# Two of the four weight sums of the last up block and of all down units, made by memory-to-memory transfers during the up product

## The chip, the cores and the metric

One core of a Trainium2 chip runs the whole kernel in one launch. The metric is device time in microseconds; lower is better. Three runs of the kernel before took 2117.33, 2120.94 and 2121.91 us, so the median is 2120.94 us.

## The reference, cut to what matters

The program is one decoder block on 512 rows of 2048 channels, in float32: a norm, an input projection, two token mixers, an output projection, and then the channel mixer, which is all that the change touches:

```
h   = rmsnorm(x) * norm2_g                 # 512 x 2048
up  = h @ ffn_w_up                         # 2048 x 12288
up  = causal depthwise conv, width 3       # per column
gate, val = split(up)
x   = x + (gelu(gate) * val) @ ffn_w_down  # 6144 x 2048
out = rmsnorm(x) * final_g
```

## The kernel before, in words

**Products.** Each matrix product of the channel mixer is cut into 2 x 2 blocks and done with seven block products in place of eight. A "unit" is one step of it: a weight block of 2 x 128 rows by 512 columns against the matching part of the activations. A unit makes seven products (`ORDER`, `SLOTS`), each in two halves of the rows and in three passes (high by high, high by low, low by high part), so 42 matmuls in line 782. 24 up blocks of 8 units (192 units, `ups`) come first, gate and value by turns, and then 88 down units: `CHUNKS` of 8, 8 and 6 row pairs, each for four column groups `n`. A last piece of the down product (two row pairs, `TAIL`) is done plainly at the end.

**What a weight needs.** A tile `q` has eight slots of 128 x 256. A weight's four quarters are loaded into slots 4 to 7 by one transfer of 512 KB from SyncE's queue, SP (`Weights.load`, line 581). VectorE then makes four sums (`Weights.sums`): slots 2 and 3 in one instruction (line 585: slots 5 and 6, each plus slot 7), slot 1 (line 586: slot 2 plus slot 6), slot 0 (line 587: slot 1 plus slot 4). Then `pair` splits slots 0 to 6 into a high and a low part: ScalarE casts (line 115), VectorE subtracts (line 116). An activation tile goes the same way (`Acts`, lines 604, 610 to 612, and line 116 as `al`); in the down product it is read back from `ad`, an array in device memory to which the value blocks write their result (line 850, from GpSimd, POOL).

**What sets the order.** From line 755 on the program order is the order of each engine. `stream` lists weights and activations in the order of use; `prepare` walks it. For entry n it issues load n+1, makes the sums of n+1, pairs n, and issues load n+2; `ready` sets it to run two units ahead of the product. `q`, the high parts and the low parts have three buffers each. So load e+3 waits on SP until VectorE has finished the pair of entry e, and between that moment and the sums of e+3 VectorE has the sums of e+2, the pair of e+1 and whatever `lazy` work lies between. `lazy` work is hung on later units by `later`: after an up block the seven `combine` steps at its end and the convolution steps of `rest` (lines 845, 848) in the units +1, +2, +4 and +5 of the next block; after a down block three sums out of PSUM (lines 895, 898, 900) at its end and pairs of `steps` (lines 902 to 909) in the units +0 to +3 of the next.

**Activations of the down product.** They are entries of the same stream, at spread-out places around each start of a chunk (`spread`, `after`): 8 for the first chunk, in units 187 to 199 counted from the first up unit, 8 in 219 to 231, 6 in 251 to 260, each prepared about two units earlier.

**POOL** issues few transfers: the writes to `ad`, and in the down product the reads and writes of the residual `xs` to and from `x2d` (lines 886 and 922, 1 MB each). Each waits in POOL's queue for what it writes.

Of the kernel before, what the change touches and what calls it, by code (L numbers as in the profile page):

```python
# [8 lines left out]
F32 = mybir.dt.float32  # L9
# [3 lines left out]
ALU = mybir.AluOpType  # L13

P = 128
# [31 lines left out]
CHUNKS = [range(0, 8), range(8, 16), range(16, 22)]  # L47
TAIL = 22
# [16 lines left out]


@with_exitstack
def hybrid_block(ctx: ExitStack, tc: tile.TileContext, x, xT, w_in, w_out, w_up, w_dn, w_dl, wab, wsT, vec, bs, vgb, fg, out):
    nc = tc.nc
    const = ctx.enter_context(tc.tile_pool(name="const", bufs=1))  # L70
    def pool(name, side, bufs=1):
# [2 lines left out]
    def psum(name, bufs):  # L74
        return tc.alloc_tile_pool(name=name, bufs=bufs, space=bass.MemoryType.PSUM, reuse_waits="tile")
# [34 lines left out]
    def col(at):  # L110
        return vc[:, at:at + 1]
# [43 lines left out]
    def sl(pair, *idx):  # L155
        return tuple(t[idx] for t in pair)
# [54 lines left out]
    def rms_rstd(dst, sums, width, n):  # L211

        m = sums.shape[-1]
        v = mx.tile([P, n], F32, name="rms_v", tag="rms_v", bufs=2)
        if m > 1:
            nc.vector.tensor_reduce(v, sums, mybir.AxisListType.X, ALU.add)
            sums = v
        else:
            sums = sums[:, :, 0]
        nc.vector.tensor_scalar(v, sums, 1.0 / width, RMS_EPS, ALU.mult, ALU.add)  # L220
        rsqrt(dst, v)
# [348 lines left out]
    def slots(name, n=8):  # L570
        return wq.tile([P, n, 256], F32, name=name, tag=name)

    class Weights:


        def __init__(self, src):
            self.src = src

        def load(self):
            self.q = slots("q")  # L580
            nc.sync.dma_start(self.q[:, 4:8], self.src)

        def sums(self):
            q = self.q
            nc.vector.tensor_tensor(q[:, 2:4], q[:, 5:7], q[:, 7:8].broadcast_to([P, 2, 256]), ALU.add)  # L585
            nc.vector.tensor_tensor(q[:, 1], q[:, 2], q[:, 6], ALU.add)  # L586
            nc.vector.tensor_tensor(q[:, 0], q[:, 1], q[:, 4], ALU.add)  # L587

# [52 lines left out]
    stream = []  # L641
# [4 lines left out]
    def rest_of_loads():  # L646
        while halves:
            halves.pop(0)()

    def prepare(upto, last=None):  # L650

        last = len(stream) - 1 if last is None else last
        for n in range(done[2], upto + 1):

            for i, step, ahead in ((0, "load", 1), (1, "sums", 1), (2, "pair", 0), (0, "load", 2)):
                for k in range(done[i], min(n + ahead, last) + 1):
                    if step == "sums":
                        rest_of_loads()
                    getattr(stream[k], step)()
                    done[i] = k + 1  # L660

    ups = [(g, v) for g in range(NG) for v in range(2)]
    units = [(w_up[g + NG * v, m], m) for g, v in ups for m in range(8)]
    starts = []
    for c in CHUNKS:
        starts.append(len(units))
        units += [(w_dn[n, p], p - c[0]) for n in range(4) for p in c]
    n_up = starts[0]

    def act_tiles(m, shape):  # L670
        a = pools["a2" if m == 7 else "a1"]
        return tuple(a.tile(shape, F32R, name=f"a{n}{m}", tag=f"a{n}{m}") for n in "hl")
# [46 lines left out]
    last_w = [Plain([w_dl[d].rearrange("p (a b) -> p a b", a=8)], half_tiles(i)) for i, d in enumerate(DORD)]  # L719
    for u, (src, _) in enumerate(units):  # L720
        place[u] = len(stream)
        stream.append(Weights(src))
        for a in after.get(u, ()):
            if a.fill is not None:
                a_place[a.m] = len(stream)
            stream.append(a)
        if u == len(units) - 5:
            stream.append(last_a)
        if u == len(units) - 2:
            stream.append(last_w[0])  # L730
    stream += last_w[1:]

    def ready(u):

        if u < 7:
            return a_place[u + 1 if u else 0]
        n = len(units)
        return place[u + 3] - 1 if u + 3 < n else place[n - 1] + max(0, u - n + 2)
# [33 lines left out]
    def product(q, p, a, w, up, first, last):  # L772
        sa, sb = SLOTS[p]
        if first:
            q[p] = qbank().rearrange("p (t n) -> p t n", t=2)
        for t in range(2):
            s, r = ((w, sb), (a, sa)) if up else ((a, sa), (w, sb))
            sh, slo = (h[:, s[1], t * P:(t + 1) * P] for h in s[0])
            rh, rlo = (h[:, r[1]] for h in r[0])
            for n, (x_, y_) in enumerate(((sh, rh), (sh, rlo), (slo, rh))):  # L780

                nc.tensor.matmul(q[p][:, t], lhsT=x_, rhs=y_, start=first and t == 0 and n == 0, stop=last and t == 1 and n == 2, skip_group_check=True)  # L782
# [3 lines left out]
    def later(step, f):  # L786
        lazy.setdefault(step, []).append(f)

    def t_tile(name, shape, bufs=1):
        return pools["t"].tile(shape, F32, name=name, tag=name, bufs=bufs)  # L790
# [4 lines left out]
    def combine(q, c1, c11, c12, c21, c22):  # L795

        tt = nc.vector.tensor_tensor
        nc.scalar.copy(c1, q[1])
        tt(c11, c1, q[2], ALU.add)  # L799
        v, w = t_tile("v", [P, 2, 256]), t_tile("w", [P, 2, 256])  # L800
        tt(v, q[6], c1, ALU.subtract)
        tt(w, q[5], v, ALU.add)
        tt(c12, w, q[3], ALU.add)
        tt(c22, w, q[7], ALU.add)
        tt(v, v, q[7], ALU.add)
        tt(c21, q[4], v, ALU.subtract)
# [3 lines left out]
    def up_block(g, val, u0):  # L810
        q = {}
        for m in range(8):
            prepare(ready(u0 + m))
            for p in ORDER:
                product(q, p, act[m], stream[place[u0 + m]].hl, True, m == 0, m == 7)
                if p == 6:
                    rest_of_loads()
            if m == 7 and u0 == 0:
                pads[:] = [t_tile(f"pad{n}", [P, 2, S + 2]) for n in range(2)]
                for t in pads:  # L820
                    nc.gpsimd.memset(t[:, :, 0:2], 0.0)
            for f in lazy.pop(u0 + m, ()):
                f()
        c1 = t_tile("c1", [P, 2, 256])
        lo, hi = slice(2, 258), slice(258, 514)
        combine(q, c1, pads[0][:, :, lo], pads[1][:, :, lo], pads[0][:, :, hi], pads[1][:, :, hi])
        if u0 == 0:
            pools["ps"].release()
            pools["tr"].release()
            pools["ps"] = psum("q1", 8)  # L830

        def tap(n, j, f):
            if val:
                dst = t_tile("cv", [P, 2, S])if j == 0 else cvs[n]
                cvs[n] = dst
            else:
                if j == 0:
                    gates[n] = t_tile("gate", [P, 2, S], 2)
                dst = gates[n]
            nc.scalar.activation(dst[:, j], pads[n][:, j, 2:2 + S], AF.Identity, bias=col(V_FB + f), scale=col(V_FW + 2 * 96 + f))  # L840

        def rest(n, j, f):
            dst = (cvs if val else gates)[n][:, j]
            for i in (1, 0):
                nc.vector.scalar_tensor_tensor(dst, pads[n][:, j, i:i + S], col(V_FW + i * 96 + f), dst, ALU.mult, ALU.add)
            if val:
                gate = gates[n][:, j]
                nc.vector.tensor_tensor(gate, gate, dst, ALU.mult)
                at = 0 if j else 2
                nc.gpsimd.dma_start(ad[2 * g + n][:, at:at + 2], gate.rearrange("p (a b) -> p a b", a=2))  # L850

        def gelu(n, j):
            t = gates[n][:, j]
            nc.scalar.activation(t, t, AF.Gelu_apprx_tanh)

        cvs = {}
        at = u0 + 8
        for i, (n, j) in enumerate(((1, 0), (1, 1), (0, 0), (0, 1))):
            f = 48 * val + 4 * g + 2 * n + j
            step = at + (0, 1, 3, 4)[i]  # L860
            later(step, lambda n=n, j=j, f=f: tap(n, j, f))
            later(step + 1, lambda n=n, j=j, f=f: rest(n, j, f))
            if not val:
                later(step + 2, lambda n=n, j=j: gelu(n, j))

    pads = []
    for b, (g, val) in enumerate(ups):
        up_block(g, val, 8 * b)
# [69 lines left out]
    for st in range(NS):  # L938
# [4 lines left out]
        for n, (i, d, lo, hi) in enumerate(pieces):  # L943
            ps = qbank()[:, 0:hi - lo]
            for f in range(4):
                at = (0 if f % 2 else 1024 // 2) + st * P
                a = sl(last_a.hl[f // 2], slice(None), slice(at, at + P))
                w = sl(last_w[i].hl[f // 2], slice(None), slice(f % 2 * 512 + lo, f % 2 * 512 + hi))
# [12 lines left out]
        v, y, u, r = (const.tile([P, 1], F32, name=f"r3{c}", tag=f"r3{c}", bufs=2) for c in "vyur")  # L961
# [7 lines left out]
        for n in order:  # L969
            _, d, lo, hi = pieces[n]  # L970
# [64 lines left out]
```

## Time and profile before

| | us |
|---|---|
| three runs | 2117.33, 2120.94, 2121.91 |
| median | 2120.94 |
| profiled execution | 2120.2 |
| its span | 2118.5 |
| TensorE busy | 2052.5 (97%) |
| VectorE busy | 1807.7 (85%) |
| ScalarE busy | 910.6 (43%) |
| GpSimd busy | 59.7 (3%) |

The profiled execution lies 0.7 us under the median, and 1.7 us of it lie around the span. Sums are made against it. The mean granted clock of TensorE was 0.985 of full speed (2.4 GHz). A matmul's duration is modelled and matmuls overlap in the pipeline, so the pace of line 782 is read from counts over a stretch, not from the duration of one.

### The profile page before, as it was taken

How to read it: one execution, taken by the hardware profiler on the slowest of the kernel's cores; microseconds unless marked ns; L12 is line 12 of the kernel's file. 1: busy time of each engine (PE TensorE's matmuls, PEld its weight loads, DVE VectorE, ACT ScalarE, POOL GpSimd, SP SyncE). 2: the span in 40 equal slices, each digit the busy share in tenths (PEclk: the TensorE clock that was granted, in tenths of full speed). 3: DMA queues.
4: the chain of work that ended last, by engine and by line, in shares of the span. 5: the costliest groups of instructions: out<-in, count | busy, mean ns of one | idle time of the engine just before them, and what ended most of it. 6: DMA issues, size and time to landing. Idle time of an engine off the chain costs nothing.

```text
span 2118.5 us, 34519 instructions
## 1 busy us (share of the span) xinstructions
PE 2052.5 (97%) x14488; PEld 1931.3 (91%) x14488; DVE 1807.7 (85%) x2345; ACT 910.6 (43%) x899; POOL 59.7 (3%) x118
## 2 busy tenths in 40 slices
PE   9999999999889999999999999999988998999998
PEld 7888888888689999999999999999988998998996
DVE  7588972745389999999999999999999999989986
ACT  6445322413264444444444444444444344444443
POOL 0000000100000000000000000000000000000000
PEclk9999999999899999999999999999999999999999
DMA  6222322434123443333333333333335454544563
GB/s 236 87 90 90 102 97 99 159 124 158 57 70 103 127 125 105 129 116 115 120 123 115 121 113 118 120 118 122 113 120 177 151 181 168 178 150 160 199 214 125
DMA packets 68604, 275.12 MB, mean 130 GB/s; under 512 B 8160, under 2 KB 8800, under 8 KB 58720
## 3 DMA queue, kind: packets, MB, share of 16 engines
q1 hardware_dynamic: 57888, 224.01, 32.6%
q0 software_dynamic: 9984, 48.24, 6.1%
q8 instruction: 113, 1.85, 0.4%
q10 hardware_dynamic: 576, 0.66, 0.1%
q14 instruction: 43, 0.35, 0.1%
HBM read 241.43 MB, written 31.46 MB: 129 GB/s over the span
## 4 chain that ended last, share of the span: by engine, by line
PE 80%; DVE 15%; DMA 3%; ACT 1%; issue 1%; SPq 0%; DVEq 0%; ACTq 0%
PE qs L782 52%; PE ps L153 9%; PE ps L151 9%; PE ps L152 9%; DVE wl L116 5%; DVE al L116 2%; DVE q L585 1%; DMA q<-w_dn 1%; DVE q L586 1%; DVE q L610 1%; DVE q L587 1%; DMA q<-w_up 1%; PE qs L152 1%; PE qs L153 1%; PE qs L151 1%
## 5 line engine op out<-in xcount | busy, mean ns | idle before, releaser
L782 PE MATMUL qs<-ah,wh 128*128 128x256 f32 x2688 | 764.6, 284 | 3.1 <-DVE pad L799 1.9
L782 PE MATMUL qs<-ah,wl 128*128 128x256 f32 x2688 | 763.2, 284 | 4.3 <-DVE wl L116 4.3
L782 PE MATMUL qs<-al,wh 128*128 128x256 f32 x2688 | 763.5, 284 | 2.9 <-DVE al L116 2.7
L115 ACT CAST wh<-q 128x1792 fp32r<-128x1792 f32 (+1 forms) x282 | 476.8, 1691 | 669.9 <-PE qs L782 472.6
L116 DVE TENSOR_TENSOR wl<-q,wh 128x1792 fp32r<-128x1792 f32 (+1 forms) x282 | 567.5, 2013 | 25.0 <-ACT wh L115 24.8
L782 PEld LDWEIGHTS qs<-ah,wl 128*128 128x128 f32 x2688 | 518.5, 193 | 4.7 <-DVE wl L116 4.7
L782 PEld LDWEIGHTS qs<-al,wh 128*128 128x128 f32 x2688 | 518.7, 193 | 3.7 <-DVE al L116 3.7
L782 PEld LDWEIGHTS qs<-ah,wh 128*128 128x128 f32 x2688 | 518.6, 193 | 3.7 <-DVE pad L799 2.1
L782 PE MATMUL qs<-wl,ah 128*128 128x256 f32 x1232 | 355.8, 289 | 16.1 <-DVE wl L116 16.0
L782 PE MATMUL qs<-wh,ah 128*128 128x256 f32 x1232 | 355.1, 288 | 9.1 <-ACT cc L894 3.5
L782 PE MATMUL qs<-wh,al 128*128 128x256 f32 x1232 | 354.4, 288 | 4.7 <-DVE al L116 4.7
L782 PEld LDWEIGHTS qs<-wl,ah 128*128 128x128 f32 x1232 | 242.5, 197 | 18.4 <-DVE wl L116 18.3
L782 PEld LDWEIGHTS qs<-wh,ah 128*128 128x128 f32 x1232 | 242.5, 197 | 10.5 <-ACT cc L894 3.9
L782 PEld LDWEIGHTS qs<-wh,al 128*128 128x128 f32 x1232 | 242.3, 197 | 5.1 <-DVE al L116 5.1
L116 DVE TENSOR_TENSOR wl<-wraw,wh 128x1024 fp32r<-128x1024 f32 (+2 forms) x105 | 118.0, 1125 | 147.1 <-ACT wh L115 146.8
L115 ACT CAST wh<-wraw 128x1024 fp32r<-128x1024 f32 (+2 forms) x105 | 102.2, 974 | 275.1 <-PE ps L152 145.3
L585 DVE TENSOR_TENSOR q<-q 128x512 f32<-128x512 f32 x280 | 191.6, 684 | 14.6 <-DMA q<-w_dn 13.1
L151 PE MATMUL ps<-xgh,wh 128*128 128x512 f32 x384 | 152.4, 397 | 0.6 <-ACT wh L115 0.5
L152 PE MATMUL ps<-xgl,wh 128*128 128x512 f32 x384 | 152.1, 397 | 0.0
L153 PE MATMUL ps<-xgh,wl 128*128 128x512 f32 x384 | 150.5, 397 | 0.0
L586 DVE TENSOR_TENSOR q<-q 128x256 f32<-128x256 f32 x280 | 119.0, 425 | 9.7
L587 DVE TENSOR_TENSOR q<-q 128x256 f32<-128x256 f32 x280 | 119.1, 425 | 9.6
(242 smaller groups left out, 2285.2 us busy)
## 6 DMA issues: line engine op xcount, KB each, us to landing
q<-w_up SPq DMA_DIRECT2D x192, 512.0 KB, 3.5
q<-w_dn SPq DMA_DIRECT2D x88, 512.0 KB, 3.5
wraw<-w_in SPq DMA_DIRECT2D x28, 1024.0 KB, 4.9
wraw<-w_out SPq DMA_DIRECT2D x16, 1024.0 KB, 4.9
ad<-gate POOLq DMA_DIRECT2D x48, 256.0 KB, 2.3
q<-ad SPq DMA_DIRECT2D x24, 512.0 KB, 3.2
xs<-x2d POOLq DMA_DIRECT2D x12, 1024.0 KB, 5.9
x2d<-xs POOLq DMA_DIRECT2D x10, 1024.0 KB, 5.1
```

Source lines behind the costliest of these rows:

```text
L115: nc.scalar.copy(h, src)
L116: nc.vector.tensor_tensor(l, src, h.bitcast(F32), ALU.subtract)
L151: nc.tensor.matmul(ps, lhsT=ah, rhs=bh, start=start, stop=False)
L152: nc.tensor.matmul(ps, lhsT=ah, rhs=bl, start=False, stop=False)
L153: nc.tensor.matmul(ps, lhsT=al, rhs=bh, start=False, stop=stop)
L585: nc.vector.tensor_tensor(q[:, 2:4], q[:, 5:7], q[:, 7:8].broadcast_to([P, 2, 256]), ALU.add)
L586: nc.vector.tensor_tensor(q[:, 1], q[:, 2], q[:, 6], ALU.add)
L587: nc.vector.tensor_tensor(q[:, 0], q[:, 1], q[:, 4], ALU.add)
L610: nc.vector.tensor_tensor(q[:, 2:4], q[:, 7:8].broadcast_to([P, 2, 256]), q[:, 5:7], ALU.subtract)
L782: nc.tensor.matmul(q[p][:, t], lhsT=x_, rhs=y_, start=first and t == 0 and n == 0, stop=last and t == 1 and n == 2, skip_group_check=True)
```

## The change

For the eight weights of the last up block (units 184 to 191) and the 88 of the down product, slots 2 and 3 are no longer made by line 585. The host hands over a second copy of the operands as `w_us` and `w_ds`: for each weight two arrays of 256 KB, one with the quarters of slots 5 and 6, one with the quarter of slot 7 twice. `make(u)`, called once in each up unit u from 0 to 191, issues one transfer from POOL, memory to memory, of 32 rows of 8 KB: for even u a copy of the first array into `made`, for odd u the second array added to what is there. After two up units the sums of one weight are done; 96 weights take 192 units. Such a weight is then loaded by two transfers, 256 KB of `made` into slots 2 and 3 (2 KB a partition) and 384 KB of the quarters into slots 4 to 6 (3 KB a partition), where one transfer of 512 KB was (4 KB a partition). Lines 586 and 587 and the pair stay as they are.

```diff
-            self.q = slots("q")
-            nc.sync.dma_start(self.q[:, 4:8], self.src)
+            self.q = q = slots("q")
+            if self.made is None:
+                nc.sync.dma_start(q[:, 4:8], self.src)
+            else:
+                nc.sync.dma_start(q[:, 2:4], self.made)
+                nc.sync.dma_start(q[:, 4:7], self.src[:, 0:3])
 
         def sums(self):
             q = self.q
-            nc.vector.tensor_tensor(q[:, 2:4], q[:, 5:7], q[:, 7:8].broadcast_to([P, 2, 256]), ALU.add)
+            if self.made is None:
+                nc.vector.tensor_tensor(q[:, 2:4], q[:, 5:7], q[:, 7:8].broadcast_to([P, 2, 256]), ALU.add)
             nc.vector.tensor_tensor(q[:, 1], q[:, 2], q[:, 6], ALU.add)
             nc.vector.tensor_tensor(q[:, 0], q[:, 1], q[:, 4], ALU.add)
...
+    sums_src = [w_us[m] for m in range(8)] + [w_ds[n, p] for c in CHUNKS for n in range(4) for p in c]
+    for k, src in enumerate(sums_src):
+        made[n_up - 8 + k] = tc.dram_tile([32, 2048], F32, name=f"made{k}")
+
+    def make(u):
+
+        k = u // 2
+        if k < len(sums_src):
+            how = {"accum_op": ALU.add, "max_dma_last_dim": 8192} if u % 2 else {"max_dma_last_dim": 8192}
+            nc.gpsimd.dma_start(made[n_up - 8 + k], sums_src[k][u % 2], **how)
...
                 if p == 6:
                     rest_of_loads()
+            make(u0 + m)
             if m == 7 and u0 == 0:
...
+        "w_us": pairs(i["ffn_w_up"][0])[23],
+        "w_ds": pairs(i["ffn_w_down"][0][:TAIL * 2 * P]),
```

## Rows read from the trace of the kernel before

**Rows 1.** Section 1 of the page: busy time, share of the span and instructions of each engine.

```profile
PE 2052.5 (97%) x14488; PEld 1931.3 (91%) x14488; DVE 1807.7 (85%) x2345; ACT 910.6 (43%) x899; POOL 59.7 (3%) x118
```

**Rows 2.** Busy time of line 782 alone, over the whole of both block products: stretch, its length, PE busy (matmuls), PEld busy (weight loads), granted clock, DMA share, GB/s.

```profile
474.00:2065.00 1591.00, 1439.08 (x11760) 1431.33 (x11760) 0.98 0.41 133
```

**Rows 3.** The same for stretches from the last two up blocks to the end of the down units, PE only: stretch, length, PE busy (matmuls), granted clock, DMA share, GB/s.

```profile
1526.00:1576.00 50.00, 44.18 (x351) 0.97 0.37 117
1576.00:1642.00 66.00, 56.33 (x414) 0.90 0.47 160
1642.00:1713.00 71.00, 70.79 (x590) 1.00 0.51 172
1713.00:1813.00 100.00, 89.06 (x702) 0.97 0.49 168
1813.00:1890.00 77.00, 76.68 (x639) 1.00 0.50 165
1890.00:1967.00 77.00, 69.83 (x554) 0.96 0.46 151
1967.00:2063.00 96.00, 95.93 (x787) 0.98 0.61 209
```

**Rows 4.** Busy time of every engine in a stretch within the up product: stretch, length, PE (matmuls), PEld, DVE, ACT, POOL, granted clock, DMA share, GB/s.

```profile
700.00:900.00 200.00, 200.00 (x1669) 200.00 (x1668) 192.23 (x244) 90.67 (x75) 5.42 (x10) 1.00 0.38 119
```

**Rows 5.** VectorE's groups by line: the sums of a weight and the low part of its pair (busy us, mean ns of one, idle time before).

```profile
L116 DVE TENSOR_TENSOR wl<-q,wh 128x1792 fp32r<-128x1792 f32 (+1 forms) x282 | 567.5, 2013 | 25.0 <-ACT wh L115 24.8
L585 DVE TENSOR_TENSOR q<-q 128x512 f32<-128x512 f32 x280 | 191.6, 684 | 14.6 <-DMA q<-w_dn 13.1 <-DMA q<-w_up 0.8
L586 DVE TENSOR_TENSOR q<-q 128x256 f32<-128x256 f32 x280 | 119.0, 425 | 9.7
```

**Rows 6.** VectorE in order of time, early in the last up block: start us, duration us, what.

```profile
1537.89 0.69 DVE L585 TENSOR_TENSOR q<-q 128x512 f32<-128x512 f32 x1
1538.62 0.43 DVE L586 TENSOR_TENSOR q<-q 128x256 f32<-128x256 f32 x1
1539.08 0.43 DVE L587 TENSOR_TENSOR q<-q 128x256 f32<-128x256 f32 x1
1539.42 2.02 DVE L116 TENSOR_TENSOR al<-q,ah 128x1792 fp32r<-128x1792 f32 x1
1541.36 1.53 DVE L845 SCALAR_TENSOR_TENSOR gate<-pad,vc,gate 128x512 f32<-128x512 f32 x2
1542.81 0.68 DVE L585 TENSOR_TENSOR q<-q 128x512 f32<-128x512 f32 x1
```

**Rows 7.** Pieces of the chain that ended last which are loads, from the last up block to the end of the third chunk's start: start us, us, what.

```profile
1571.66 3.45 DMA q<-w_dn
1608.67 3.65 DMA q<-w_dn
1630.63 7.95 DMA q<-w_dn
1642.21 17.90 PE qs L782 x147
...
1746.53 5.31 DMA q<-ad
1800.61 5.22 DMA q<-w_dn
...
1933.49 3.57 DMA q<-w_dn
```

**Rows 8.** DMA queues (packets, MB, share of 16 engines' span) and issues (KB each, median us from issue to landing).

```profile
q1 hardware_dynamic: 57888, 224.01, 32.6%
q0 software_dynamic: 9984, 48.24, 6.1%
q<-w_dn SPq DMA_DIRECT2D x88, 512.0 KB, 3.5
wraw<-w_in SPq DMA_DIRECT2D x28, 1024.0 KB, 4.9
```

**Rows 9.** SP's queue in order of time: one weight load (start us, us that it held the queue).

```profile
1554.73 0.33 SPq L581 DMA_DIRECT2D q<-w_up  x1
```

**Rows 10.** VectorE in order of time in the middle of the up product, one step of a gate block's convolution and what follows it: start us, duration us, what.

```profile
1300.75 1.53 DVE L845 SCALAR_TENSOR_TENSOR gate<-pad,vc,gate 128x512 f32<-128x512 f32 x2
1302.19 0.69 DVE L585 TENSOR_TENSOR q<-q 128x512 f32<-128x512 f32 x1
1302.91 0.42 DVE L586 TENSOR_TENSOR q<-q 128x256 f32<-128x256 f32 x1
1303.38 0.42 DVE L587 TENSOR_TENSOR q<-q 128x256 f32<-128x256 f32 x1
1303.72 2.02 DVE L116 TENSOR_TENSOR wl<-q,wh 128x1792 fp32r<-128x1792 f32 x1
1305.65 0.68 DVE L585 TENSOR_TENSOR q<-q 128x512 f32<-128x512 f32 x1
```

**Rows 11.** POOL in order of time: the last write of the residual ahead of the up product, the first clearing in it, and a write of a value block's result (start us, us, what, idle time before it and what ended that).

```profile
563.14 0.53 POOL L560 DMA_DIRECT2D x2d<-x  x1 [21.23 <-DVE x L520]
595.00 0.14 POOL L821 MEMSET pad<- 128x4 f32 x2 [31.33 <-PE tr L688]
...
1499.19 0.54 POOL L850 DMA_DIRECT2D ad<-gate  x1 [59.75 <-DVE gate L848]
```

More of the change, by code (lines that the diff above doesn't have):

```diff
@@ L67, in hybrid_block @@
 @with_exitstack
-def hybrid_block(ctx: ExitStack, tc: tile.TileContext, x, xT, w_in, w_out, w_up, w_dn, w_dl, wab, wsT, vec, bs, vgb, fg, out):
+def hybrid_block(ctx: ExitStack, tc: tile.TileContext, x, xT, w_in, w_out, w_up, w_dn, w_us, w_ds, w_dl, wab, wsT, vec, bs, vgb, fg, out):
     nc = tc.nc
@@ L573, in hybrid_block, with __init__ @@
     class Weights:
-        def __init__(self, src):
-            self.src = src
+        def __init__(self, src, made=None):
+            self.src, self.made = src, made
         def load(self):
-            self.q = slots("q")
-            nc.sync.dma_start(self.q[:, 4:8], self.src)
+            self.q = q = slots("q")
[4 more added lines that the diff above has]
+                nc.sync.dma_start(q[:, 4:7], self.src[:, 0:3])
         def sums(self):
             q = self.q
-            nc.vector.tensor_tensor(q[:, 2:4], q[:, 5:7], q[:, 7:8].broadcast_to([P, 2, 256]), ALU.add)
+            if self.made is None:
+                nc.vector.tensor_tensor(q[:, 2:4], q[:, 5:7], q[:, 7:8].broadcast_to([P, 2, 256]), ALU.add)
             nc.vector.tensor_tensor(q[:, 1], q[:, 2], q[:, 6], ALU.add)
@@ L664, in hybrid_block @@
     starts = []
+    made = {}
     for c in CHUNKS:
@@ L721, in hybrid_block @@
         place[u] = len(stream)
-        stream.append(Weights(src))
+        stream.append(Weights(src, made[u].rearrange("(p b) (c d e) -> (p b c) d e", p=32, c=4, d=2) if u in made else None))
         for a in after.get(u, ()):
@@ L1002, in quarters, with pairs @@
         return c(np.stack([b[:, :, :, 0, 1], b[:, :, :, 0, 0], b[:, :, :, 1, 1], b[:, :, :, 1, 0]], axis=3))
+    def pairs(w):
+        q = quarters(w)
+        return c(np.stack([q[:, :, :, 1:3], q[:, :, :, [3, 3]]], axis=2)).reshape(*q.shape[:2], 2, 32, 2048)
     vec = np.concatenate(
```

## The prediction, made before the changed kernel was seen

> **What bounds the kernel now.** I read the page's engine line first, then line 782 over stretches, then the chain, and last VectorE (DVE) and the queues in order of time. The engine line gives PE 97% and DVE 85% [rows 1], an average that hides the stage concerned. Line 782 has 11760 matmuls in the 1591 us of both block products [rows 2], 42 for each of 280 units. In the middle of the up product 1669 of them pass in 200 us without a gap [rows 4]: 0.120 us each, 5.04 us a unit. That stage is bound by PE, yet DVE is busy 192.2 of the 200 us, so it has 3.9% to spare, 3.1 us in 16 units (80.6 us).
>
> By the same pace I read what each later stretch loses: its length less its matmuls times 0.12 [rows 3]. 1526 to 1576: 50 - 42.1 = 7.9. 1576 to 1642: 66 - 49.7 = 16.3. 1713 to 1813: 100 - 84.2 = 15.8. 1890 to 1967: 77 - 66.5 = 10.5. Together 50.5 us; the stretches between them lose under 2 us each. The four losing stretches are three places, A, B and C, the starts of the three chunks, where activations of the down product go through DVE beside the weights. In them the chain runs along DVE, broken by loads [rows 7]. The granted clock is 1.00 (the 2.4 GHz level) where PE never waits, and 0.90 in mean in the stretch where it waits longest.
>
> **What the change removes.** 96 executions of line 585 at 684 ns [rows 5], 65.7 us of DVE. In sequence one is worth 0.72 us, the step from its start to that of line 586 [rows 6]. The sums of a weight then take 0.80 us in place of 1.53 (to the start of the pair, same rows), a pair 1.94. Only sums made while DVE sets the end count: by the order of `prepare`, 16 weights in A (units 187 to 202), 16 in B (219 to 234), 12 in C (251 to 262), so 44 x 0.72 = 31.7 us. The other 52 free DVE time where PE sets the pace: nothing.
>
> **What takes part of it back: the load.** Three buffers of `q` mean that load e+3 starts when the pair of e ends, and DVE reaches the sums of e+3 after one lot of sums and one pair, plus whatever lazy work lies between. Without lazy work that was 1.53 + 1.94 = 3.47 us, and the load there takes 3.45 to 3.65 [rows 7]: they are balanced to a tenth. After the change DVE is there in 2.74 us (3.47 if the sums between are an activation's), and the load is bigger: 640 KB in two transfers.
>
> The length of the new load, L, no row shows. Lower end, bytes alone: 1024 KB land in 4.9, 512 KB in 3.5 [rows 8], so 128 KB more cost 0.35: 3.45 + 0.35 = 3.8. Upper end, packets alone: a load of 1024 KB makes as many packets (224 MB in 57888 is 3.9 KB each [rows 8], so 256) as two transfers of 128 partitions; with the second issue, 0.33 us on SP [rows 9], 4.9 + 0.33 = 5.2. Ours has 256 packets of 2 and 3 KB, nearer to the bytes; the first transfer's data covers the second's issue. I take 4.1.
>
> The Trainium skill (DMA: Bandwidth & Descriptors, Anatomy of one DMA) fits a transfer as about 2.0 us plus bytes over 436 GB/s; as an estimate from it 128 KB more cost 0.3, L is 3.75 and the gain would be 21.6 before the deductions below. The rows' slope, 0.35, is a little steeper.
>
> Now the waits, by walking entry by entry through A, B and C. A window holds at least 1.2 us of lazy work in most units, and 2.74 + 1.3 = 4.04 covers L. Not covered are six weights with bare windows (194, 196, 199; 224, 234; 256), each L - 2.74 = 1.36, together 8.2; four whose window holds an activation's sums (188, 225, 232, 257), each L - 3.47 = 0.63, together 2.5; three that follow directly on a weight that waited (226, 233, 258), 0.72 each, and one activation, loaded in 3.45 against 2.74, 0.7: together 2.9. Sum 13.6 us. 31.7 - 13.6 = 18.1: about 6.1 in A, 6.0 in B, 5.9 in C, each below what that place loses, so PE can take it.
>
> **Smaller terms.** Loads beside 1 MB transfers of `xs` take 5.2 to 8.0 us [rows 7]. Two weight loads there grow by 0.4 and their sums shrink by 0.7; two activation loads (the one shown in B and its like in C) are the same and DVE reaches them 0.7 sooner, which is lost. Net 1 us lost. SP issues 96 more transfers of 0.33 us, hidden in the 2.7 us between two loads.
>
> **POOL.** It gains 192 issues of about 0.54 us [rows 11], 104 us, and is idle 97%. The addition waits in its queue for the copy to land. By issue 0.54, landing up to 3.5 and issue 0.54 a weight takes some 5 us, so eight in 16 units hold it 40 of 80 us. Queued behind are the writes to `ad`, delayed by up to one such wait, 4 us; their `gate` buffers are wanted again six units (30 us) later. The clearing of the pads stands behind the first eight transfers; POOL has 31 us between the write at 563 and the clearing [rows 11] and needs 20. Without that cover (over 8 us a weight) the first block starts late by the excess, once. A `made` of unit 184 + k is finished by unit 2k + 1, and its load is asked for about unit 181 + k: never late.
>
> **The up product.** The transfers share the 16 DMA engines with weight loads there. Per engine a copy is 16 KB; q0 moved 48.24 MB in 6.1% of 16 engines' span and q1 224.01 MB in 32.6% [rows 8], 43 and 49 us x engine per MB, so 0.7 to 0.8 us. For an addition no row exists: from nothing beyond a copy (0.75), if reading its target is hidden, to three passes (2.4). I take two, 1.5. A load of 3.45 beside it becomes 4.95. The shortest window in an up block is sums, pair and one step of 1.45: 1302.19 - 1300.75 + 3.46 = 4.9 us [rows 10]; in a value block 5.6. So an addition just fits, and the 3.1 us to spare absorb the rest; with jitter I charge 1 to 2 us.
>
> The Trainium skill (DMA: Bandwidth & Descriptors, Issuing engines are not separate DMA queues) speaks against the change here: transfers of all queues interleave on the same 16 engines. It gives no price for an addition, and no row of this trace shows one.
>
> **Sum.** 18.1 - 1 - 2 = 15 us. The profiled execution took 2120.2, 0.7 below the median of the runs: 2105 there, 2106 as a median.
>
> **Rivals.**
> 1. The load takes all of it. With one transfer more and 256 packets L may be 4.8 or more. Then the windows with lazy work no longer cover: 6 x 2.06 + 4 x 1.33 + 2.9 = 20.6, and about 17 windows of 4.1 lose 0.7 each, 11.9: 32.5, the whole gain. The time is 2121. At L = 5.2 it is about 11 us worse. For it: balance already at 3.45, so any growth counts double. Against it: small packets. Chance 0.18.
> 2. Contention in the up product: slower. If an addition holds an engine 2.4 us, a load beside it takes 5.85, DVE waits 0.95 in a window of 4.9, and PE, with only 3.1 us of DVE time to spare per 16 units, is passed. Eight additions in 16 units: 7.6 - 3.1 = 4.5, in some 11.5 such stretches 52 us; less the 17 gained, 2155. It decides from about 2.0 us an addition: 8 x 0.55 - 3.1 = 1.3, times 11.5 is 15. For it: DVE is 96% busy there; after each four `ad` writes POOL runs ahead, so transfers bunch. Against: the stage's DMA share is only 0.38 [rows 4], and `prepare` runs two units ahead. Chance 0.20.
> 3. The loads stay at 3.45. Then waits are 6 x 0.71 + 2.9 = 7.2, the gain 24.5, and with a steadier clock in A up to 30: 2096, at best 2090. For it: both transfers are in flight together. Against: more bytes. Chance 0.15.
>
> **How the numbers follow.** The forecast, 2098 to 2116, has 0.47. An 80% range takes in rivals 3 and 1 and the near end of rival 2: 2090 to 2132. About 0.2% (4 us) is what a measurement of this kernel can tell from no change. Faster by over that: 0.47 + 0.15 less 0.03 of the forecast's edge, 0.59. Within: 0.13 of rival 1, 0.03 of the edge and 0.01 of rival 2's mild forms: 0.17. Slower: 0.19 of rival 2 and 0.05 of rival 1: 0.24.
>
> **What would show it.** In the changed profile line 585 runs 184 times. Weight loads of the down units land about 4.1 us after the first issue. DVE's idle time on those loads in A to C grows from 13 us [rows 5] to some 20 to 25, and the matmuls of A to C take 18 us less. In the up product PE stays at 1669 matmuls in 200 us. I am wrong if PE falls below that (rival 2), or if the chain in A to C is made of loads (rival 1).

## The result, and the profile after

The changed kernel took 2107.73 us as a median of four runs (2103.72 to 2108.02) against 2120.68 for four of the kernel before: ratio 0.9935, 95% interval 0.9923 to 0.9948. Two later sets of five gave 0.9925 (0.9913 to 0.9938) and 0.9937 (0.9924 to 0.9951). The forecast was 2106 as a median; the profiled execution took 2107.67 where 2105 was forecast.

The engine line, which answers to [rows 1]:

```profile
PE 2048.9 (97%) x14488; PEld 1928.0 (92%) x14488; DVE 1746.8 (83%) x2249; ACT 911.5 (43%) x899; POOL 185.9 (9%) x310
```

DVE has 96 instructions and 61 us less, POOL 192 instructions and 126 us more. The product line, 782 before, is line 800 now; over the whole of both block products, as in [rows 2]:

```profile
474.00:2053.00 1579.00, 1435.05 (x11760) 1428.07 (x11760) 0.98 0.56 173
```

The stretches that answer to [rows 3] (length, PE busy and matmuls, granted clock, DMA share, GB/s), cut at the same points of the chain:

```profile
1528.00:1576.00 48.00, 43.07 (x355) 1.00 0.65 190
1576.00:1624.00 48.00, 40.15 (x291) 0.88 0.47 157
1624.00:1717.00 93.00, 93.00 (x757) 0.97 0.58 205
1717.00:1805.00 88.00, 78.94 (x632) 0.98 0.59 202
1805.00:1890.00 85.00, 85.00 (x708) 1.00 0.54 188
1890.00:1957.00 67.00, 63.82 (x515) 0.97 0.54 189
```

Length less 0.12 us a matmul: 5.4, 13.1, 12.2 and 5.2 in the four losing stretches, 35.9 us where [rows 3] gave 50.5. The middle of the up product, as in [rows 4], with all transfers running:

```profile
700.00:900.00 200.00, 200.00 (x1669) 200.00 (x1669) 191.96 (x245) 89.44 (x74) 34.22 (x54) 1.00 0.63 175
```

The same 1669 matmuls, though the DMA share went from 0.38 to 0.63. VectorE's groups, as in [rows 5] (line 590 was 585, 591 was 586), and its idle time by what ended it, 1520 to 2060 us (engine, line, what it waited for: us in total, times, longest):

```profile
L590 DVE TENSOR_TENSOR q<-q 128x512 f32<-128x512 f32 x184 | 126.1, 685 | 6.4 <-DMA q<-w_up 6.2
```

```profile
DVE wl L116 <- ACT wh L115: 44.1, 37, 3.0
DVE q L591 <- DMA q<-w_dn: 20.1, 18, 3.1
DVE q L615 <- DMA q<-ad: 6.6, 5, 2.5
DVE q L591 <- DMA q<-w_up: 3.1, 3, 1.7
...
DVE xs L914 <- DMA xs<-x2d: 1.4, 1, 1.4
```

The same view of the kernel before:

```profile
DVE q L585 <- DMA q<-w_dn: 13.1, 12, 2.8
DVE wl L116 <- ACT wh L115: 9.5, 8, 3.0
DVE q L610 <- DMA q<-ad: 2.5, 2, 2.1
```

So waits on loads went from 15.6 us in 14 places to 31.2 in 27. Not all of that was given back: a wait of VectorE costs time only in the starts, and TensorE (PE) runs without a gap from 1624 to 1717 and from 1805 to 1890 us. The same view of the changed kernel for the three starts alone (1528 to 1624, 1717 to 1805 and 1890 to 1957 us):

```profile
DVE q L591 <- DMA q<-w_dn: 3.3, 4, 1.5
DVE q L591 <- DMA q<-w_up: 2.5, 2, 1.7
DVE q L615 <- DMA q<-ad: 1.2, 1, 1.2
...
DVE q L591 <- DMA q<-w_dn: 7.5, 4, 3.1
DVE q L615 <- DMA q<-ad: 2.7, 2, 2.1
...
DVE q L615 <- DMA q<-ad: 2.7, 2, 2.5
DVE q L591 <- DMA q<-w_dn: 1.9, 2, 1.1
```

And of the kernel before (1526 to 1642, 1713 to 1813 and 1890 to 1967 us):

```profile
DVE q L585 <- DMA q<-w_dn: 3.0, 2, 2.8
...
DVE q L585 <- DMA q<-w_dn: 3.0, 2, 1.7
DVE q L610 <- DMA q<-ad: 0.5, 1, 0.5
...
DVE q L610 <- DMA q<-ad: 2.1, 1, 2.1
DVE q L585 <- DMA q<-w_dn: 0.2, 1, 0.2
```

In the starts the waits went from 8.8 us in 7 places to 21.8 in 17: 13.0 us given back. The waits on line 115, ScalarE's cast, went from 9.5 to 44.1 us, and 42.8 of these lie between the starts and behind the last. There the cast in its turn waits for a buffer that TensorE still reads:

```profile
1717.00 1.69 ACT L115 CAST wh<-q 128x1792 fp32r<-128x1792 f32 x1 [3.35 <-PE qs L800]
...
1718.72 2.03 DVE L116 TENSOR_TENSOR wl<-q,wh 128x1792 fp32r<-128x1792 f32 x1 [0.29 <-ACT wh L115]
```

So most of what the sums outside the starts took, 52 x 0.72 = 37 us, became idle time of VectorE. The chain shows the loads, as in [rows 7]; here are pieces from the last up block to the second start, with the issue of the first of the two transfers in the line ahead of a load:

```profile
1535.74 0.33 SPq L584
...
1536.11 4.63 DMA q<-w_up
...
1552.78 4.76 DMA q<-ad
...
1572.95 0.32 SPq L584
...
1573.31 3.35 DMA q<-w_dn
...
1588.12 3.19 DMA q<-w_dn
...
1608.61 3.70 DMA q<-w_dn
...
1742.59 7.56 DMA q<-ad
...
1795.85 6.12 DMA q<-w_dn
```

Beside the transfers a load here took 5.0 us from its first issue (1535.74 to 1540.74). Once the last of them, issued at 1552, is over, the loads shown in A take 3.6 to 4.1 (1572.95 to 1576.66 is 3.7). The last two lines, in B, are loads beside the 1 MB transfers of the residual.

The gain can be laid out by unit: the start of every 42nd matmul of the product line, in order of time, in us later (+) or earlier (-) than in the profiled execution of before.

```
unit      0      12     184    204    236    268    last
after   -0.05  +2.84  +2.84  -1.04  -5.07  -12.02  -12.02
```

Up product, units 0 to 184, +2.9, A (184 to 204) -3.9, B (to 236) -4.0, C (to 268) -7.0, what follows the last unit -0.5: -12.5 in the span.

### The profile page after: what moved, and what is told of

Read it like the earlier page. It is cut to its first block, busy times and chain, and to the rows that moved or that the text cites. A ratio compares the mean times of both kernels' runs of the same rounds, so it can differ in the third digit from the quotient of the medians.

```text
span 2106.0 us, 34882 instructions
## 1 busy us (share of the span) xinstructions
PE 2048.9 (97%) x14488; PEld 1928.0 (92%) x14488; DVE 1746.8 (83%) x2249; ACT 911.5 (43%) x899; POOL 185.9 (9%) x310
## 4 chain that ended last, share of the span: by engine, by line
PE 84%; DVE 10%; DMA 4%; issue 1%; ACT 1%; SPq 0%; DVEq 0%; ACTq 0%
PE qs L800 56%; PE ps L153 9%; PE ps L152 9%; PE ps L151 9%; DVE wl L116 3%; DVE al L116 2%; DMA q<-ad 1%; DMA q<-w_dn 1%; DMA q<-w_up 1%; DVE q L591 1%; DVE q L615 1%; PE qs L152 1%; PE qs L153 1%; PE qs L151 1%; DVE q L592 0%
## 5 line engine op out<-in xcount | busy, mean ns | idle before, releaser
L800 PEld LDWEIGHTS qs<-wh,ah 128*128 128x128 f32 x1232 | 240.9, 196 | 12.2 <-ACT cc L913 4.9
L591 DVE TENSOR_TENSOR q<-q 128x256 f32<-128x256 f32 x280 | 118.6, 424 | 29.7 <-DMA q<-w_dn 20.1
L686 POOL DMA_DIRECT2D made<-w_ds x176 | 115.3, 755 | 283.0 <-DMA made<-w_ds 273.8
L590 DVE TENSOR_TENSOR q<-q 128x512 f32<-128x512 f32 x184 | 126.1, 685 | 6.4 <-DMA q<-w_up 6.2
```

Source lines behind the costliest of these rows:

```text
L686: nc.gpsimd.dma_start(made[n_up - 8 + k], sums_src[k][u % 2], **how)
```

## Experiments

Theory A: the removed sums are worth their 0.72 us each in the three starts, less what VectorE then waits for longer loads; the transfers cost only where VectorE is late, in the first up block and in the last. Rivals are named with each run.

**1. No transfers.** The two slots come straight from the first operand array.

```diff
-            make(u0 + m)
-        made[n_up - 8 + k] = tc.dram_tile([32, 2048], F32, name=f"made{k}")
+        made[n_up - 8 + k] = src[0]
```

> Leaves out the memory-to-memory transfers: the two slots are loaded straight from the first operand array, so the product of the last up block and of the down units is not the reference's. Loads (two, 640 KB) and VectorE work are those of the changed kernel (2107.7). Theory A (the transfers cost something only where VectorE is late: the first two up blocks, 2.8 us, and the last up block, where loads took 4.8 to 5.1 us): 2102, with the shift of the first up blocks gone and some 3 us more gained in A. Rival B (the transfers are hidden, and what is missing of the 31.7 us is lost to the loads alone): 2107 to 2108.

2105.07 us, ratio 0.9920 (0.9905 to 0.9935): between the two. By unit: +0.4 in the first blocks (0 to 12), A -6.1, B -4.9, C -6.1. A moves as theory A has it, 2.2 us better without transfers where some 3 were expected.

**2. Transfers alone.** Nobody reads what they make; loads and sums as before.

```diff
-        stream.append(Weights(src, made[u].rearrange("(p b) (c d e) -> (p b c) d e", p=32, c=4, d=2) if u in made else None))
+        stream.append(Weights(src))
```

> The 192 transfers are issued as in the changed kernel, but nobody reads what they make: loads and sums are those of the kernel before (2120.7). Theory A: slower than before by 2.8 us in the first two up blocks and 1 to 3 us in the last one: 2124 to 2126, and nothing in the 20 blocks between. Rival B: 2120 to 2121. If contention were as I feared (an addition takes an engine 2.4 us), 2155.

2124.66 us, ratio 1.0018 (1.0008 to 1.0027), so 3.9 us slower and as theory A has it. By unit +1.3 from 0 to 12 (2.8 were expected), 0.0 from 12 to 184, +1.3 in A.

**3. One load for two.** Five slots lie together in memory, and one transfer of 640 KB brings them.

```diff
-                nc.sync.dma_start(q[:, 2:4], self.made)
-                nc.sync.dma_start(q[:, 4:7], self.src[:, 0:3])
+                nc.sync.dma_start(q[:, 2:7], self.made)
```

> As no_make, but the 640 KB come in one transfer of five slots (5 KB a partition) from an array in which they lie together; the sums of slots 2 and 3 are left out as there. Theory A (bytes set the length of a load): 3.7 to 3.8 us as with two transfers, and the time of no_make within 1 us. Rival C (the second issue, 0.36 us after the first, is what lengthens it): loads of 3.4 us, nine bare windows shorter by 0.36, 3 us less than no_make.

2105.15 us against 2105.07 for the two transfers: the second issue costs nothing that shows. The issue lists (KB each, median us from issue to landing) of no_make, the two transfers, and then of one_load:

```profile
q<-w_dn SPq DMA_DIRECT2D x88, 384.0 KB, 3.4
q<-w_ds SPq DMA_DIRECT2D x88, 256.0 KB, 2.7
```

```profile
q<-w_ds SPq DMA_DIRECT2D x88, 640.0 KB, 3.9
```

The second is issued 0.36 us after the first, so it lands 3.8 us after it; one transfer of the same bytes takes 3.9. Rival C is out.

**4. Longer loads.** As no_make, with slot 7 loaded too.

```diff
-                nc.sync.dma_start(q[:, 4:7], self.src[:, 0:3])
+                nc.sync.dma_start(q[:, 4:8], self.src)
```

> As no_make (2105.1; no transfers from memory to memory, the two slots hold the first operand alone), but the second transfer brings slot 7 too, which nobody reads: 768 KB a weight in place of 640. By the slope of the loads that is 0.35 us more for each. Theory (VectorE in the starts goes at the pace of the loads where a window is bare): 13 windows x 0.35 = 4.5 us slower than no_make, 2109 to 2110, all of it in the three starts. Rival F (the loads are not what bounds): 2105.

2112.58 us, 7.5 more than no_make where 4.5 was expected. The issue list gives 3.7 for the second transfer, 0.3 more than in no_make. VectorE's waits on loads from 1520 to 2060 us:

```profile
q<-w_dn SPq DMA_DIRECT2D x88, 512.0 KB, 3.7
```

```profile
DVE q L591 <- DMA q<-w_dn: 40.8, 27, 4.6
...
DVE q L615 <- DMA q<-ad: 5.7, 4, 2.5
DVE q L591 <- DMA q<-w_up: 4.3, 3, 2.7
```

By unit A -2.9, B -0.1, C -4.8. B, worth 4.9 us in no_make, is gone with 0.3 us more per load. In the three starts alone the waits on loads grew from 19.7 us in 16 places (no_make) to 28.1 in 19, 8.4 us for the 7.5 of the runs, so the loads bound the starts. The added wait is not an even 0.3: 3.4 of the 8.4 us lie at two neighbouring weights of B, 232 and 233, whose loads run beside the 1 MB transfers (2.3 at one of them). Rival F is out.

**5. Only the weights of the starts.** 47 weights are made, in units 16 to 109, so no transfer runs beside the first or the last up block.

```diff
+    wanted = [u for u in range(n_up - 8, len(units)) if 186 <= u <= 202 or 218 <= u <= 234 or 250 <= u <= 262]
-        k = u // 2
-        if k < len(sums_src):
+        k = (u - 16) // 2
+        if 0 <= k < len(wanted):
```

> Computes the reference. Only 47 weights (units 186 to 202, 218 to 234, 250 to 262, the three starts) are made by transfers, 94 of them, one per up unit from 16 to 109; the other 49 are loaded and summed as before. Theory A: the first two up blocks and the last one are free of transfers, and weights outside the starts gain nothing anyway: as no_make, about 2102, faster than the changed kernel by 5. Rival D (the sums saved between the starts let VectorE get ahead and count too): 2106 or more.

2103.12 us, ratio 0.9918 (0.9901 to 0.9936). Once more, beside the changed kernel on one chip:

> The changed kernel once more, to stand on one chip with the next two: 2107 to 2108, ratio to before 0.9935.

> The kernel of starts_only once more. Theory A (transfers beside the first and the last up block cost, weights between the starts gain nothing): 3 to 5 us faster than after_again. Rival D (weights between the starts count): the same or slower.

2106.07 (ratio 0.9925) and 2105.51 (0.9919, 0.9906 to 0.9933): the intervals overlap widely, and the 3 to 5 us do not show in the runs. In the profiles A reads -5.3 and -5.8 against -3.9 and -3.4, as theory A has it, but C -4.8 and -5.8 against -7.0 and -6.1. A third execution of the changed kernel (experiment 8) has A -4.1 and C -5.6, so A stands apart and C does not.

The times decide nothing between theory A and rival D, but the traces speak against D. It needs VectorE to enter a start further ahead, and VectorE is as far ahead as the buffers let it in either kernel: ahead of B and of C it waits for a cast in starts_only (until 1717.9 and 1891.7) as in the changed kernel (1718.7 and 1892.6). With the other 49 sums back, its waits on the cast are 11.1 us in starts_again in place of 44.1:

```profile
DVE wl L116 <- ACT wh L115: 11.1, 14, 2.6
```

**6. Without the bare weights.** As 5, but the six weights that the walk called bare are loaded and summed as before.

```diff
+    wanted = [u for u in wanted if u not in (194, 196, 199, 224, 234, 256)]
```

> As starts_only, without the six weights that I counted as bare (194, 196, 199, 224, 234, 256), where VectorE waits for the load after the change: these are loaded and summed as before. Theory (where the load is the bound a removed sum is worth nothing, the load gives it back): within 1.5 us of starts_again, to either side. Rival E (each removed sum in the starts is worth its 0.72 us): 4.3 us slower than starts_again.

2103.45 us, ratio 0.9914 (0.9901 to 0.9928): 2.1 us under starts_again, so outside the 1.5 that were expected, though the intervals overlap. Rival E, which has 4.3 over it, is out: at these six weights, where the load is the bound, the removed sum was worth nothing.

**7. Each transfer twice**, the second into a spare array.

```diff
             nc.gpsimd.dma_start(made[n_up - 8 + k], sums_src[k][u % 2], **how)
+            nc.gpsimd.dma_start(spare[k], sums_src[k][u % 2], **how)
```

> As the changed kernel (computes the reference), but each of the 192 transfers is issued a second time, into a spare array that nobody reads. Two additions then lie together on the 16 engines, 3.2 us each engine by the 1.6 us that the q0 share gives for one. My arithmetic of rival 2 (a load beside them takes 3.45 + 3.2 = 6.65, VectorE waits 1.75 in a window of 4.9, eight times in 16 units, less 3.1 us to spare, 11.5 such stretches): 10.9 x 11.5 = 125 us slower, some 2230. Rival G (the loads share the engines packet by packet and lose less, or two units of lead take it up): under 2125, with the up blocks' pace still 1669 matmuls in 200 us in most of the stage.

2152.05 us, ratio 1.0143 (1.0124 to 1.0161): slower by 44 than the changed kernel. Neither number holds. The stage does break, as rival 2 has it, but at a quarter of the price that I gave the up product. A stretch of the up product with its matmuls, and VectorE's waits from 560 to 1530 us:

```profile
900.00:1100.00 200.00, 195.57 (x1615) 194.26 (x1615) 184.69 (x234) 89.36 (x75) 56.97 (x89) 1.00 0.79 221
```

```profile
DVE q L590 <- DMA q<-w_up: 42.9, 32, 4.4
```

32 waits on loads, 42.9 us. By unit this execution is 4.9 us late at unit 0 and 38.9 at unit 184, the changed kernel 2.8 there and on time at unit 0. So some 31 us more are lost in the up product. I had eight additions in 16 units delay a load; 32 waits in 24 blocks are under three in 16.

**8. The better version against the changed one**, on one chip.

> The kernel of not_bare once more (41 weights made by transfers, from unit 16 on, none of the six bare ones). 2103 to 2105 if its gain over the changed kernel (2106 to 2108) is real, ratio to before 0.991 to 0.992.

> The changed kernel, on the same chip as not_bare_again: 2106 to 2108, ratio 0.993.

2104.85 (2104.17 to 2106.19) and 2108.10 us (2106.95 to 2111.27), ratios 0.9922 (0.9909 to 0.9934) and 0.9937 (0.9924 to 0.9951). No run of the one reaches a run of the other in this set: 3.2 us, 0.15%, with 82 transfers in place of 192. It beats the kernel before clearly and the changed one by little: over all sets the runs (2102.31 to 2106.45 against 2103.72 to 2111.27) and the intervals against before overlap.

## Why the prediction was right, point by point

**What bounds the kernel.** Right: the 12.5 us of the span came from the three starts (14.9 us by unit). Between the starts (units 204 to 219 and 236 to 251) nothing moves, and the 52 other sums turned into waits for casts.

**What is removed.** Right for one sum: line 590 runs 184 times, and the sums of a weight take 0.80 us (line 591 to line 116: 1545.02 to 1545.82 in the trace). The count of 44 is a little high. In A TensorE no longer waits from unit 200 on, so the sums of weights 201 and 202 count for nothing. Up to unit 200 the rest adds up: 14 sums are 10.1 us, the waits grew from 0.2 to 7.0, and A gained 3.2.

**What the load takes back.** The total came out, 13.0 us more waiting in the starts against 13.6 + 1, and that was in part luck. L is 3.6 to 4.1 in four of the six bare windows (194, 196, 199 and 256) and 3.7 in the median, near the lower end of 3.8, where I took 4.1 for the packets; 256 small packets cost no more than their bytes (experiment 3). With L alone put right, the ten terms that hold it would have been 4 us smaller and the forecast gain 19 us in place of 15. The walk was too short by about as much. Experiment 4 shows it: there a load takes the 4.1 of my walk (0.36 + 3.7), the waits in the starts are 19.3 us longer than before (28.1 for 8.8) where the walk has 13.6 + 1, and the gain without any transfers was 9.2 us (2112.58 against 2121.83) where it leaves 18.1 - 1 = 17.1. The 17 waits are nearly as many as I had counted, with the two activations of the smaller terms, but not all the same ones: the weights 190 and 193 and two more activations wait and were not counted, the weights 225, 234 and 257 were and do not wait. The 4.04 us of a window with lazy work do not quite cover 4.1 either, as the walk had it.

The fit of the Trainium skill (DMA: Bandwidth & Descriptors, Anatomy of one DMA) comes close to the increment: 0.3 us for 128 KB by an estimate from it, and 3.45 to 3.7 or 3.8 was measured. The page states the fit for transfers issued from GpSimd, and these loads are issued from SP.

**Loads beside 1 MB transfers, and act loads.** Under-counted: the waits on `ad`, all in the starts, went from 2.5 to 6.6 us, and I had charged 1. It is part of the 13.0. Weight 224 waits 2.7 us in place of 1.3 and weight 233 3.1 in place of 1.7, both with such a transfer beside the load. The wait of 1.4 us on the residual's read is new, but lies where TensorE runs without a gap.

**Where.** A gave 3.9, B 4.0 and C 7.0, 14.9 in all, for 6.1, 6.0 and 5.9. In A the last transfers still run, issued until 1552, and loads take 5.0; I had looked for contention in the up product's steady part only. Experiments 1 and 2 give 1.3 to 2.2 us for it. So the steps that were off are the reach of the walk and the contention in A, and a load shorter than I took made up for most of them.

**POOL.** Right that it is no bound. It holds back nothing that anyone waits for; the clearing of the pads began at 595.09, as in [rows 11]. The first eight transfers do stand ahead of it, but not in the 31 us in front of it, where I had put them: they run in the first 30 us of the kernel, the first at 1.4 us, and the next at 595.16, right behind the clearing.

**The up product.** I charged 1 to 2 us; 2.9 are lost, all in the first two blocks, where activations pass through VectorE and the chain runs along it, as in A. One load of the chain there, and the same one in the kernel before:

```profile
610.77 5.04 DMA q<-w_up
```

```profile
610.67 3.45 DMA q<-w_up
```

From unit 0 to 12 four executions with these transfers lose 1.0 to 2.9 us, the one with each of them twice some 2, and seven without them between -1.9 and +0.4. In the 172 units after that this execution loses nothing. The addition's engine time is near what I took: POOL's queue (q0) rose from 6.1% to 17.0% of the span,

```profile
q0 software_dynamic: 19200, 98.58, 17.0%
```

358 us less 129, over 192 transfers 1.2 us an engine each, so 1.6 for an addition if a copy takes 0.75. A load of 3.45 beside it would take 5.05, a little over the shortest window of 4.9, and the executions of the changed kernel lose 0.3 us at most between units 12 and 184; experiment 7 shows that twice as much costs time. The Trainium skill's rule that all queues interleave on the same 16 engines (DMA: Bandwidth & Descriptors, Issuing engines are not separate DMA queues) agrees with the longer loads here: 5.0 us beside transfers in A and in the first block, a median of 4.5 for the up weights in experiment 7. In the steady part it costs nothing.

**The rivals.** Rival 1 (the load takes all) did not come, and was close: experiment 4 shows that 0.3 us more on each load halves the gain. Rival 2's price was about four times too high by experiment 7, where 32 loads were waited for and my arithmetic had eight in 16 units, 96 in all. Rival 3 would have needed the loads to stay at 3.45.

Left open: executions that are the same up to there begin unit 0 up to 3 us apart, and C alone reads -5.6 to -7.0 in three executions of the changed kernel, which blurs single comparisons by unit. How much of the gain came through TensorE's clock was not separated: PE was busy 4.0 us less for the same 11760 matmuls, and the granted clock in the first stretch of A was 1.00 where it had been 0.97.

## What to carry to other kernels

Before taking work off the busiest engine, find what is as late as that work: here a load without lazy work in front of it had 3.47 us of cover and took 3.45, so a shorter sum bought a wait for the load, and only about half of the removed time (14.9 of 31.7 us) came out. Count a window's cover from the trace, entry by entry, and test it by making the load longer, which cost 7.5 us for 0.3 us a load. Count waits only where the waiting engine sets the end: of 31.2 us of waits on loads, 21.8 lay there. Background transfers were free where the consumer was ahead, up to a point that experiment 7 passes, and cost where it was late. Moving them to stretches with slack and making only what is used where it counts gained 3.2 us in the one set that separates the two.

## What the runs showed of the hardware that was not expected

Two transfers of 256 and 384 KB issued 0.36 us apart landed 3.8 us after the first issue, one of 640 KB 3.9: splitting a load into two cost nothing here. And in the middle of the up product (700 to 900 us) the DMA share rose from 0.38 to 0.63 and the matmuls kept their pace, 1669 in 200 us, while in experiment 7 they fell to 1615 in 200 us at 0.79 (900 to 1100 us) and the up product lost 31 us more over its 24 blocks.
